# Splitting W_o's quadrant sums and W_A's pieces once, early, and keeping the halves in DRAM

## The chip, the cores and the metric

The kernel runs on one core of a Trainium2 chip. The metric is the device time of one execution in microseconds (us). Of the kernel before there are three runs: 1529.68, 1530.45 (the median) and 1532.38 us. Beside the times there is one profiled execution, whose trace gives every instruction of every engine and every DMA.

The engines are named as in the profile: PE is the tensor engine (PEld its weight loads), DVE the vector engine, ACT the scalar engine, POOL the GpSimd engine, and SP the sync engine, whose work here is to issue DMAs. Each engine runs its instructions in the order of its own queue.

## The reference

One layer of a streaming encoder on 2048 prompt tokens and 32 sample tokens, width 1024, all in float32:

```python
h = rmsnorm(x, ln_g)
(q, k, v, gate_a, b_gate, c_gate, u_in, gate_c, merge_a, merge_c) = split(h @ w_in)
attn = chunked sliding-window attention(q, k, v) with sinks      # 8 q heads, 2 kv heads
y_a = (attn * silu(gate_a)) @ w_attn_out                         # W_A, 512 -> 1024
y_c = (b_gate * conv3(c_gate * u_in) * silu(gate_c)) @ w_conv_out  # W_B
r = x + (sigmoid(merge_a) * y_a + sigmoid(merge_c) * y_c) @ w_o    # W_o, 1024 x 1024
out = r + sigmoid(r @ w_ple_gate) * (p @ w_ple_proj)               # W_pg, W_pp
```

The caches of k and v and the last rows of the convolution's input are outputs too.

## The kernel before, in words

**Halves.** Every matmul is made of three: an operand is split into a high half (a cast by ACT to the matmul's own float32 form) and a low half (source minus high half, by DVE), and high x high, high x low and low x high are added up in one bank. `split` (L228) does this for a tile. A weight piece is a tile of 128 x 512 (256 KB in float32); its two halves lie together in a tile `w` of 512 KB, of which there are five (`WB`).

**Seven products.** The large matrix products are computed in Strassen's way with seven products of quadrants instead of eight, numbered 1 to 7. Products 1, 2 and 4 use a weight quadrant as it is; 7, 5, 6 and 3 use sums of quadrants, named `sc`, `a21`, `a11` and `a12` in the code, and kept at places 0 to 3 (`WS`, L338).

**First phase (some 0 to 850 us of the trace).** The combined projection `h @ W_in`, by 21 groups `g` of output columns: of the first token half (steps `(0, g, product)`), then of the second. In steps whose key stands in `sums_at` (L1201), `quad_sums(x, n)` (L368) is called for the second phase: it loads the four quadrants of columns `n` of W_o (`x = UO`, 50) or W_pg (`x = UPG`, 58), makes the four sums by four adds on DVE and stores them to DRAM (`quad_sum`, `qs` in the profile) by four DMAs on POOL. Its five tiles come from the pool of temporaries `tp`. This phase is written in program order, but its start and the second phase are issued in an order that the kernel's own planner finds when the program is built: it keeps clocks for the engines (`now`, `busy`), costs per instruction (L104, L120) and counts of free tiles (`live`, `limit`), and issues a step when it fits. Between these, the framework's scheduler orders the first phase's instructions by when their tiles come free.

**Second phase.** `plan` (L307 to L318) lists its units: `yB` (W_B), `pp` (W_pp), `yA` (W_A, by token blocks 0 to 3 and column pieces), and `B` units, the seven products of W_o and W_pg for the first token half (named `b050_...` and `b058_...`: half, matrix, columns, product) and for the second (`b150_...`, `b158_...`). Attention (L1343) runs beside them, tile by tile, started at fixed amounts of PE work; its transposes and products stand between the units' matmuls on PE. Rows of activations are split into `xb` pairs (L1645). Outputs are evicted into tiles `c` (`big_done`, L1698) and combined on DVE, then brought together with x or r by an accumulating DMA on POOL and stored by SP.

**Weights of the second phase.** `worder` (L325) lists every weight piece in the order of use. `next_loads` (L1924) runs whenever the planner's clock moves: it lets SP load raw pieces, up to 11 ahead of the one in use (`LOOK`), into one of eight tiles `wr` (tag `wf`): from `in_wu` where a piece is a quadrant, from `quad_sum` where it is a sum (L1954). When one has landed, a `w` tile is free and ACT is not busy, `split_w` (L1910) splits it. W_A's pieces are used once per token block, so each is loaded and split four times; each sum of W_o twice.

## Time and profile before

| | |
|---|---|
| Median of three runs | 1530.45 us |
| Profiled execution, its own time | 1533.35 us |
| Span from first to last instruction | 1531.6 us |
| Mean granted PE clock | 0.991 |
| PE, DVE, ACT, POOL busy | 98%, 80%, 53%, 24% |
| DMA moved | 346.89 MB, mean 226 GB/s |

A busy share is the time in which at least one instruction of the engine was in flight. Matmuls overlap each other, so a duration in a PE row is longer than the distance between two of them; the distance is read from counts (so many matmuls in so many us). In rows of waits stand the engine, tile and line that waited, what it waited for, the sum, the number of waits and the longest. In rows of stretches each engine's busy time is followed by its number of instructions; then come the granted clock, the mean busy share of the 16 DMA engines and the rate. [...]

### The profile page before, as it was taken

The numbers are of one execution on the slowest core, as the hardware profiler recorded it, in microseconds if no ns is written. First come the engines' busy times: TensorE is split into PE (matmuls) and PEld (weight loads), VectorE is DVE, ScalarE is ACT, GpSimd is POOL, SyncE is SP. The second block draws the span as 40 slices with busy tenths as digits, with TensorE's granted clock in tenths as the row PEclk, the third lists the DMA queues.
The fourth block names the chain that finished last, engine by engine and source line by source line (L and its number), as shares of the span: only waits on it lengthen the run. The fifth ranks groups of instructions, "written<-read, shape, count | busy, mean of one in ns | idle before, by whom it ended". The sixth has DMA issues, their size and how long they took to land.

```text
span 1531.6 us, 27944 instructions
## 1 busy us (share of the span) xinstructions
PE 1500.7 (98%) x9553; PEld 1355.8 (89%) x9553; DVE 1227.2 (80%) x2330; ACT 818.2 (53%) x1933; POOL 370.5 (24%) x534
## 2 busy tenths in 40 slices
...
GB/s 340 151 276 342 313 295 216 282 344 266 241 279 257 315 149 195 112 132 119 175 192 187 265 234 205 210 186 231 239 127 184 187 128 300 312 240 145 254 143 288
DMA packets 199231, 346.89 MB, mean 226 GB/s; under 512 B 23728, under 2 KB 57072, under 8 KB 199088
## 3 DMA queue, kind: packets, MB, share of 16 engines
...
HBM read 227.66 MB, written 117.46 MB: 225 GB/s over the span
## 4 chain that ended last, share of the span: by engine, by line
PE 38%; DVE 7%; ACT 3%; DMA 2%; issue 2%; SPq 0%; ACTq 0%; DVEq 0%
PE b L158 17%; PE yB L158 5%; PE yA L158 5%; PE O L158 2%; PE S L158 2%; DVE c L158 1%; PE la L749 1%; PE pp L158 1%; PE a L611 1%; PE a L613 1%; PE a L616 1%; PE PT L158 1%; DVE w L158 1%; DVE xb_l L158 1%; DVE tk L158 1%
## 5 line engine op out<-in xcount | busy, mean ns | idle before, releaser
L158 PE MATMUL b<-xb_h,w 128*128 128x264 f32 (+1 forms) x1344 | 315.3, 326 | 7.2 <-DVE c L158 4.5
L158 PEld LDWEIGHTS b<-xb_h,w 128*128 128x128 f32 x1344 | 225.1, 190 | 27.6 <-DVE c L158 4.2
L613 PE MATMUL a<-x_l,w 128*128 128x264 f32 (+1 forms) x744 | 228.1, 320 | 0.0
L611 PE MATMUL a<-x_h,w 128*128 128x264 f32 (+1 forms) x744 | 227.1, 319 | 0.0
L158 PE MATMUL b<-xb_l,w 128*128 128x264 f32 (+1 forms) x672 | 218.4, 325 | 0.8 <-DVE xb_l L158 0.8
L616 PE MATMUL a<-x_h,w 128*128 128x264 f32 (+1 forms) x744 | 201.6, 320 | 0.0
L229 ACT CAST w<-wr 128x512 fp32r<-128x512 f32 (+1 forms) x180 | 110.2, 619 | 105.7 <-PE c L616 35.4
L230 DVE TENSOR_TENSOR w<-wr,w 128x512 fp32r<-128x512 f32 (+1 forms) x180 | 136.1, 767 | 33.9 <-ACT w L229 32.7
L158 ACT CAST w<-wr 128x512 fp32r<-128x512 f32 x168 | 103.5, 623 | 105.7 <-PE b L158 53.0
L611 PEld LDWEIGHTS a<-x_h,w 128*128 128x128 f32 x744 | 139.9, 188 | 10.5
L613 PEld LDWEIGHTS a<-x_l,w 128*128 128x128 f32 x744 | 139.7, 188 | 10.7
L158 PEld LDWEIGHTS b<-xb_l,w 128*128 128x128 f32 x672 | 127.8, 190 | 10.8 <-DVE xb_l L158 1.6
L616 PEld LDWEIGHTS a<-x_h,w 128*128 128x128 f32 x744 | 125.0, 188 | 10.7
L158 DVE TENSOR_TENSOR w<-wr,w 128x512 fp32r<-128x512 f32 x168 | 117.8, 706 | 14.1 <-ACT w L158 13.4
L749 PE MATMUL la<-x_h,w 128*128 128x264 f32 x516 | 112.2, 285 | 1.9 <-ACT w L229 1.2
L613 PE MATMUL c<-x_l,w 128*128 128x512 f32 (+1 forms) x336 | 110.7, 339 | 0.0
L611 PE MATMUL c<-x_h,w 128*128 128x512 f32 (+1 forms) x336 | 110.6, 340 | 0.0
L229 ACT CAST w<-a 128x512 fp32r<-128x512 f32 x82 | 49.7, 620 | 98.1 <-DVE a L360 31.5
L616 PE MATMUL c<-x_h,w 128*128 128x512 f32 (+1 forms) x336 | 100.4, 340 | 0.0
L810 DVE SCALAR_TENSOR_TENSOR u<-u,c 128x264 f32<-128x264 f32 (+1 forms) x125 | 59.4, 506 | 44.5 <-ACT u L805 30.0
L158 PE MATMUL yB<-ycs_h,w 128*128 128x264 f32 (+1 forms) x384 | 91.0, 326 | 0.0
L805 ACT COPY u<-a 128x264 f32<-128x264 f32 (+1 forms) x114 | 47.4, 437 | 80.7 <-PE a L616 80.7
...
## 6 DMA issues: line engine op xcount, KB each, us to landing
wr<-in_wu SPq DMA_DIRECT2D x177, 256.0 KB, 4.1
a<-in_wu SPq DMA_DIRECT2D x116, 256.0 KB, 5.3
wr<-ws SPq DMA_DIRECT2D x74, 256.0 KB, 3.5
wr<-qs SPq DMA_DIRECT2D x64, 256.0 KB, 3.9
ws<-a POOLq DMA_DIRECT2D x63, 256.0 KB, 4.0
qs<-a POOLq DMA_DIRECT2D x24, 256.0 KB, 5.8
...
```

The lines of the kernel that those rows point to most:

```text
L158: return f(**kw)
L229: nc.scalar.copy(out=hi, in_=src)
L230: nc.vector.tensor_tensor(out=lo, in0=src, in1=hi.bitcast(F32), op=sub)
L611: nc.tensor.matmul(out=ps[:, :cn], lhsT=w[:, 0, k], rhs=x[0][:, c0:c0 + cn], start=first and k == 0, stop=False, skip_group_check=True)
L613: nc.tensor.matmul(out=ps[:, :cn], lhsT=w[:, 0, k], rhs=x[1][:, c0:c0 + cn], start=False, stop=False, skip_group_check=True)
L616: nc.tensor.matmul(out=ps[:, :cn], lhsT=w[:, 1, k], rhs=x[0][:, c0:c0 + cn], start=False, stop=k == 3, skip_group_check=True)
L749: nc.tensor.matmul(out=ps[:, :m], lhsT=w[:, a, k], rhs=r[:, cols], start=q in "ABG" and j == 0 and e == 0, stop=j == 1 and e == 2, skip_gr ...
L805: nc.scalar.copy(out=t[:, c0:c0 + cn], in_=ps[:, :cn])
L810: nc.vector.scalar_tensor_tensor(out=t[:, c0:c0 + cn], in0=t[:, c0:c0 + cn], scalar=-1.0, in1=ps[:, :cn], op0=mul, op1=sub)
```

## The change

`quad_sum` of W_o now keeps two halves per sum, 128 x 2 x 512, and a new array `wa_split` keeps the eight W_A pieces in the same way (`wa` in the profile). `quad_sums` takes its tiles from a new pool of five tiles (`zp`) that lives during the first phase, and is done in two parts: the loads at step `(0, g, 6)`, the adds, splits and stores at `(0, g, 7)`. For W_o each sum is split at once (`store_split`: an ACT cast into a temporary, a DVE subtraction in place) and stored by two DMAs of 256 KB; W_pg's sums are stored unsplit. `piece_split` loads, splits and stores a W_A piece. W_o's sums are called for at g = 1, 3, 5, 7, W_pg's now at 9, 11, 13, 15, W_A's pieces at 2, 4, ... 16; before, the eight sums stood at g = 1 to 8.

In the second phase, `stored` says of a piece whether its halves lie in DRAM: the 32 uses of W_A's pieces and the 32 uses of W_o's sums. For these `next_loads` skips the raw load, and when a `w` tile is free SP loads both halves into it by one DMA of 512 KB; `split_w` is not called.

The order of the instructions moves in three places that matter. The first is the start-up, on SP and on DVE. `wr` are raw weight pieces, `a0` the quadrants of the first group's sums, `b1` and `sq1` rows of x and their squares, `a11_50_0` and the like the quadrants of W_o's first columns. SP before:

```order
L158 DMA wr7_405<-in_wu 128x512
L158 DMA wr8_426<-in_wu 128x512
L158 DMA a0_0_488<-in_wu 128x512
L158 DMA a0_1_489<-in_wu 128x512
L158 DMA a0_2_490<-in_wu 128x512
L158 DMA a0_3_491<-in_wu 128x512
L158 DMA wr9_644<-in_wu 128x512
L158 DMA wr10_652<-in_wu 128x512
```

and with the change:

```order
L158 DMA wr7_413<-in_wu 128x512
L158 DMA wr8_434<-in_wu 128x512
L372 DMA a11_50_0_1125<-in_wu 128x512
L372 DMA a21_50_0_1127<-in_wu 128x512
L158 DMA a0_0_496<-in_wu 128x512
L372 DMA a22_50_0_1129<-in_wu 128x512
L372 DMA a12_50_0_1131<-in_wu 128x512
L158 DMA a0_1_497<-in_wu 128x512
L158 DMA a0_2_498<-in_wu 128x512
L158 DMA a0_3_499<-in_wu 128x512
L372 DMA wa_0_1299<-in_wu 128x512
L158 DMA wr9_652<-in_wu 128x512
```

W_o's four quadrants and the first W_A piece now stand among the start-up's loads; before, the quadrants' loads came fifteen loads behind `wr9`, and no W_A piece was loaded in this phase. DVE before, at the same place:

```order
L158 TENSOR_TENSOR sq1_0_466<-sq1_0_466,sq1_4_560 128x512
L158 TENSOR_TENSOR w5_606<-wr5_309,w5_606 128x512
L158 TENSOR_TENSOR w6_610<-wr6_376,w6_610 128x512
L158 TENSOR_TENSOR w7_615<-wr7_405,w7_615 128x512
L158 TENSOR_TENSOR sc0_636<-a0_0_488,a0_1_489 128x512
L158 TENSOR_TENSOR sq1_0_466<-sq1_0_466,sq1_5_570 128x512
L158 TENSOR_TENSOR a0_1_489<-a0_1_489,a0_2_490 128x512
L158 TENSOR_TENSOR sq1_0_466<-sq1_0_466,sq1_6_582 128x512
L158 TENSOR_TENSOR a0_0_488<-a0_0_488,a0_1_489 128x512
L158 TENSOR_TENSOR sq1_0_466<-sq1_0_466,sq1_7_594 128x512
```

and with the change:

```order
L158 TENSOR_TENSOR sq1_0_474<-sq1_0_474,sq1_3_555 128x512
L387 TENSOR_TENSOR a21_50_0_1127<-a21_50_0_1127,a22_50_0_1129 128x512
L158 TENSOR_TENSOR sq1_0_474<-sq1_0_474,sq1_4_568 128x512
L158 TENSOR_TENSOR w5_614<-wr5_317,w5_614 128x512
L158 TENSOR_TENSOR w6_618<-wr6_384,w6_618 128x512
L158 TENSOR_TENSOR w7_623<-wr7_413,w7_623 128x512
L387 TENSOR_TENSOR a11_50_0_1125<-a11_50_0_1125,a21_50_0_1127 128x512
L158 TENSOR_TENSOR sc0_644<-a0_0_496,a0_1_497 128x512
L158 TENSOR_TENSOR sq1_0_474<-sq1_0_474,sq1_5_578 128x512
L387 TENSOR_TENSOR a12_50_0_1131<-a12_50_0_1131,a11_50_0_1125 128x512
L158 TENSOR_TENSOR a0_1_497<-a0_1_497,a0_2_498 128x512
L158 TENSOR_TENSOR sq1_0_474<-sq1_0_474,sq1_6_590 128x512
```

One add (`sc_50_0`) stands one row ahead of these; `sq1_7` follows two rows behind. The four adds of W_o's first sums have come in ahead of it.

The second place is W_o of the first token half. `nm` and `tt` are steps of attention, `w396` a weight's low half, `xb050_6_3_l` the low half of an activation row. DVE before:

```order
L158 SCALAR_TENSOR_TENSOR tk0_3_12693<-tk0_3_12693,tk1_3_13382 128x512
L158 TENSOR_REDUCE nm_20_13665<-S_20_0_13629 128x2
L158 TENSOR_REDUCE nm_20_13665<-S_20_1_13634 128x2
L158 TENSOR_TENSOR w396_13654<-wr396_13343,w396_13654 128x512
L158 TENSOR_TENSOR tt2_3_13658<-pq2_3_13639,ab2_3_13647 128x1024
L158 TENSOR_TENSOR tt2_3_13658<-pkv2_3_13644,ab2_3_13647 128x256
L158 TENSOR_REDUCE ss2_3_13678<-sq_10098 128x10
L158 TENSOR_TENSOR c11_050_3_2_12927<-c11_050_3_2_12927,b050_3_1_0_13618 128x512
L158 SCALAR_TENSOR_TENSOR xb050_6_3_l_13692<-tk0_3_12693,xb050_6_3_h_13691 128x512
```

and with the change:

```order
L158 TENSOR_REDUCE nm_20_13691<-S_20_1_13678 128x2
L158 TENSOR_TENSOR tk1_3_13452<-tk1_7_13531,tk1_3_13452 128x512
L158 SCALAR_TENSOR_TENSOR tk0_3_12781<-tk0_3_12781,tk1_3_13452 128x512
L158 TENSOR_TENSOR c11_050_2_2_12988<-c11_050_2_2_12988,b050_2_1_0_13653 128x512
L158 TENSOR_TENSOR tt2_3_13725<-pq2_3_13707,ab2_3_13715 128x1024
L158 TENSOR_TENSOR tt2_3_13725<-pkv2_3_13712,ab2_3_13715 128x256
L158 TENSOR_REDUCE ss2_3_13747<-sq_10230 128x10
L158 TENSOR_TENSOR c11_050_3_2_13020<-c11_050_3_2_13020,b050_3_1_0_13701 128x512
L158 RECIPROCAL se_20_13717<-se_20_13717 128x4
L158 SCALAR_TENSOR_TENSOR xb050_6_3_l_13736<-tk0_3_12781,xb050_6_3_h_13735 128x512
```

The weight's split ahead of `tt2_3` is gone. The planner, whose engines have less to do, also puts attention elsewhere. PE before, where the sample tile's probabilities are transposed (`PT_s`):

```order
L158 MATMUL b058_0_1_0_14530<-xb058_6_2_l_14612,w415_14470 128x512
L158 MATMUL b058_0_1_0_14530<-xb058_6_2_h_14611,w415_14470 128x512
L158 MATMUL PT_s_0_14685<-cst_69,Ps_14521 128x128 x2
L158 MATMUL PT_s_0_14685<-cst_69,Ps_14521 64x128
L158 MATMUL b058_0_1_0_14530<-xb058_6_3_h_14645,w415_14470 128x512
```

and with the change:

```order
L158 MATMUL b050_3_5_0_14372<-xb050_5_2_h_13969,w406_14181 128x512
L158 MATMUL PT_s_0_14412<-cst_69,Ps_14283 128x128 x2
L158 MATMUL PT_s_0_14412<-cst_69,Ps_14283 64x128
L158 MATMUL b050_3_5_0_14372<-xb050_5_2_l_13970,w406_14181 128x512
L158 MATMUL b050_3_5_0_14372<-xb050_5_2_h_13969,w406_14181 128x512
```

`PT_s` stood among W_pg's units (`b058`) and stands now among W_o's (`b050`).

The third place is SP where the second token half begins; `w441` to `w444` are the W_A pieces of units `yA2`, `tk2` their rows, `out_yT` stores of results. Before:

```order
L158 DMA wr447_15755<-in_wu 128x512
L158 DMA wr448_15765<-in_wu 128x512
L158 DMA out_yT<-c11_058_0_1_14559 128x512
L158 DMA wr449_15786<-in_wu 128x512
L158 DMA tk2_4_15791<-z_t0_4_104 128x528
L158 DMA wr450_15795<-in_wu 128x512
L158 DMA out_yT<-c11_058_1_1_14609 128x512
L158 DMA out_yT<-c11_058_2_1_14802 128x512
L158 DMA tk2_5_15847<-z_t0_5_105 128x528
L158 DMA wr451_15849<-in_wu 128x512
```

and with the change:

```order
L158 DMA w441_15826<-wa4_149 128x1024
L158 DMA pp0_3_15845<-z_pp7_91 128x512
L158 DMA wr449_15847<-in_wu 128x512
L158 DMA out_yT<-c11_058_0_1_14679 128x512
L158 DMA w442_15856<-wa5_150 128x1024
L158 DMA tk2_4_15879<-z_t0_4_104 128x528
L158 DMA wr450_15881<-in_wu 128x512
L158 DMA w443_15886<-wa6_151 128x1024
L158 DMA out_yT<-c11_058_1_1_14725 128x512
L158 DMA tk2_5_15922<-z_t0_5_105 128x528
L158 DMA wr451_15924<-in_wu 128x512
L158 DMA w444_15930<-wa7_152 128x1024
```

Loads of 128 x 1024 into `w` tiles now stand between the rows and the stores; the raw pieces of `yA2` that were loaded ahead of this place are gone.

The diff:

```diff
--- before.py
+++ after.py
@@ -363,18 +363,45 @@
         for p, i in WS.items():
             nc.gpsimd.dma_start(out=wsum[g][:, i], in_=sums[g][p])
 
-    quad_sum = {(x, n): dram.tile([P, 4, 4, P], F32, tag=f"qs{x}_{n}", name=f"qs{x}_{n}") for x in (UO, UPG) for n in range(4)}
+    quad_sum = {(x, n): dram.tile([P, 4, 1 + (x == UO), 4 * P], F32, tag=f"qs{x}_{n}", name=f"qs{x}_{n}")
+                for x in (UO, UPG) for n in range(4)}
+    wa_split = [dram.tile([P, 2, 4 * P], F32, tag=f"wa{n}", name=f"wa{n}") for n in range(8)]
+
+    def quad_load(name, u, e):
+        t = zp.tile([P, 4 * P], F32, tag="z", name=name)
+        nc.sync.dma_start(out=t.rearrange("p (a b) -> p a b", a=4), in_=wu[u, :, 4 * e:4 * e + 4, :])
+        return t
+
+    def store_split(dst, t, name):
+        h = tmp(f"h{name}", F32R)[:, :512]
+        split(h, t.bitcast(F32R), t)
+        nc.gpsimd.dma_start(out=dst[:, 0], in_=h.bitcast(F32))
+        nc.gpsimd.dma_start(out=dst[:, 1], in_=t)
 
     def quad_sums(x, n):
-        t = {}
-        for name, u, e in (("a11", n, 0), ("a21", n + 4, 0), ("a22", n + 4, 1), ("a12", n, 1)):
-            t[name] = tmp(f"{name}_{x}_{n}")[:, :512].rearrange("p (a b) -> p a b", a=4)
-            nc.sync.dma_start(out=t[name], in_=wu[x + u, :, 4 * e:4 * e + 4, :])
-        t["sc"] = tmp(f"sc_{x}_{n}")[:, :512].rearrange("p (a b) -> p a b", a=4)
+        t = {name: quad_load(f"{name}_{x}_{n}", x + u, e)
+             for name, u, e in (("a11", n, 0), ("a21", n + 4, 0), ("a22", n + 4, 1), ("a12", n, 1))}
+        yield
+        t["sc"] = zp.tile([P, 4 * P], F32, tag="z", name=f"sc_{x}_{n}")
         for o, v, w in (("sc", "a11", "a21"), ("a21", "a21", "a22"), ("a11", "a11", "a21"), ("a12", "a12", "a11")):
             nc.vector.tensor_tensor(out=t[o], in0=t[v], in1=t[w], op=add)
         for p, o in ((7, "sc"), (5, "a21"), (6, "a11"), (3, "a12")):
-            nc.gpsimd.dma_start(out=quad_sum[x, n][:, WS[p]], in_=t[o])
+            if x == UO:
+                store_split(quad_sum[x, n][:, WS[p]], t[o], f"{p}_{x}_{n}")
+            else:
+                nc.gpsimd.dma_start(out=quad_sum[x, n][:, WS[p], 0], in_=t[o])
+
+    def piece_split(n):
+        t = quad_load(f"wa_{n}", UY + n, 0)
+        yield
+        store_split(wa_split[n], t, f"wa_{n}")
+
+    def stored(key):
+        if key[0] == "q" and key[3] == 0:
+            return wa_split[key[2] - UY]
+        if key[0] == "B" and key[2] == UO and key[4] in WS:
+            return quad_sum[key[2:4]][:, WS[key[4]]]
+        return None
 
     def raw_key(key):
         if key[0] == "q":
@@ -1198,7 +1225,12 @@
         refills[at_step[at_]] = p
     after = {at_step[1, pairs_[9], 2, "C"]: sets[0]}
     after.update({at_step[1, sets[i - 1][-1], 5]: sets[i] for i in range(1, len(sets))})
-    sums_at = {(0, 1 + 2 * n + e, 6): (x, n) for n in range(4) for e, x in enumerate((UO, UPG))}
+    zpool = tc.tile_pool(name="zpool", bufs=5)
+    zp = zpool.__enter__()
+    sums_at = {(0, 1 + 2 * n, 6): quad_sums(UO, n) for n in range(4)}
+    sums_at.update({(0, 9 + 2 * n, 6): quad_sums(UPG, n) for n in range(4)})
+    sums_at.update({(0, 2 + 2 * n, 6): piece_split(n) for n in range(8)})
+    sums_at.update({(0, g, 7): v for (_, g, _), v in sums_at.items()})
     prep = [at_step[0, g, 7] for g in range(7, G)]
     for i, todo in enumerate(steps):
         if i < NS:
@@ -1214,7 +1246,7 @@
         if i in prep:
             next(X1, None)
         if todo[0] in sums_at:
-            quad_sums(*sums_at[todo[0]])
+            next(sums_at[todo[0]], None)
         if i in after:
             load_second_products(after[i])
         if i in refills:
@@ -1224,6 +1256,7 @@
             refill(refills[i])
     nc.gpsimd.dma_start(out=cpo, in_=halo)
     nc.gpsimd.dma_start(out=cso, in_=halo_out)
+    zpool.__exit__(None, None, None)
     xpool.__exit__(None, None, None)
 
 
@@ -1941,6 +1974,9 @@
 
         while n_load[0] < min(len(worder), used[0] + LOOK) and busy["Y"] < now[0] + 0.5:
             i = n_load[0]
+            if stored(worder[i]) is not None:
+                n_load[0] += 1
+                continue
             fin[0] = 0.0
             if room["wf"] < 1:
                 break
@@ -1951,16 +1987,27 @@
                 uu, e = raw_key(key)
                 eY.dma_start(out=t, in_=wu[uu, :, 4 * e:4 * e + 4, :])
             else:
-                eY.dma_start(out=t, in_=quad_sum[key[2:4]][:, WS[key[4]]])
+                eY.dma_start(out=t, in_=quad_sum[key[2:4]][:, WS[key[4]], 0].rearrange("p (a b) -> p a b", a=4))
             raw_of[i] = t
             landed[i] = fin[0] + 0.5
             n_load[0] += 1
         while n_split[0] < len(worder) and room["w"] > 0:
             i = n_split[0]
-            if landed.get(i, 1e9) > now[0] or busy["S"] >= now[0] + (0.3 if i > used[0] + 2 else 1.5):
-                break
-            room["w"] -= 1
-            go(split_w(i))
+            src = stored(worder[i])
+            if src is not None:
+                if busy["Y"] >= now[0] + 0.5:
+                    break
+                room["w"] -= 1
+                w = wp.tile([P, 2, 4, P], F32R, tag="w", name=f"w{i}")
+                W2[i] = w[:, 0], w[:, 1]
+                fin[0] = 0.0
+                eY.dma_start(out=w.bitcast(F32).rearrange("p a b c -> p a (b c)"), in_=src)
+                w_ready[i] = fin[0] + 0.5
+            else:
+                if landed.get(i, 1e9) > now[0] or busy["S"] >= now[0] + (0.3 if i > used[0] + 2 else 1.5):
+                    break
+                room["w"] -= 1
+                go(split_w(i))
             n_split[0] += 1
 
     work = [0.0]
```

## The prediction

> **What bounds the kernel now.** I read the page's head first, then busy time by stretches, then the waits of the tensor engine (PE) in the stretches where it is not full, then the place of one wait.
>
> ```profile
> span 1531.6 us, 27944 instructions
> ...
> PE 1500.7 (98%) x9553; PEld 1355.8 (89%) x9553; DVE 1227.2 (80%) x2330; ACT 818.2 (53%) x1933; POOL 370.5 (24%) x534
> ```
>
> PE is busy for 1500.7 of 1531.6 us. The change removes no matmul, so it can only win from some 31 us of idle PE and from time at half clock. The next rows (us, busy time by engine, clock, DMA share, GB/s) tell where these lie.
>
> ```profile
> core 0: us, PE busy (x) PEld busy (x) DVE busy (x) ACT busy (x) POOL busy (x), PEclk, DMA share, GB/s
> 50.00:450.00 400.00, 399.91 (x1736) 322.65 (x1735) 308.23 (x508) 174.78 (x328) 109.76 (x203) 1.00 0.79 276
> 1021.00:1195.00 174.00, 168.13 (x900) 141.44 (x899) 155.29 (x301) 115.52 (x331) 46.38 (x50) 0.99 0.75 199
> 1195.00:1311.00 116.00, 108.69 (x552) 90.34 (x551) 106.22 (x206) 83.37 (x231) 24.70 (x25) 0.94 0.75 213
> 1311.00:1385.00 74.00, 74.00 (x608) 73.91 (x607) 53.83 (x101) 34.23 (x74) 13.84 (x17) 1.00 0.93 259
> 1385.00:1432.00 47.00, 47.00 (x389) 47.00 (x388) 38.92 (x76) 20.33 (x36) 6.91 (x8) 1.00 0.70 173
> 1432.00:1525.00 93.00, 93.00 (x765) 93.00 (x765) 73.46 (x135) 44.12 (x83) 13.81 (x16) 1.00 0.82 232
> ```
>
> 1021 to 1195 holds W_A and W_o of the first token half (yA0, yA1, b50), 1195 to 1311 its W_pg (b58), 1311 to 1432 W_A and W_o of the second half. The first phase's first half (50 to 450) and the second half of the tokens lose nothing. The loss is 5.87 us in 1021 to 1195 and 7.31 in 1195 to 1311, beside half clock: 0.01 x 174 and 0.06 x 116 of clock, about 2 and 7 us at full-rate equivalent, partly inside the same gaps. Exactly there VectorE (DVE) is 89% and 92% busy, against 77 to 83% where PE is full. What ended PE's gaps, in the first of these stretches and in the second:
>
> ```profile
> PE b L158 <- ACT xb_h L158: 2.8, 1, 2.8
> PE pq L158 <- ACT E L158: 1.4, 1, 1.4
> PE b L158 <- DVE c L158: 0.9, 1, 0.9
> PE PT L158 <- ACT P L158: 0.5, 1, 0.5
> PE b L158 <- DVE xb_l L158: 0.3, 1, 0.3
> ```
>
> ```profile
> PE b L158 <- DVE c L158: 3.6, 2, 3.3
> PE PT_s L158 <- ACT Ps L158: 3.2, 1, 3.2
> PE b L158 <- DVE xb_l L158: 0.5, 1, 0.5
> ```
>
> Half of them name ScalarE (ACT), but the timeline around the 2.8 us shows that ACT itself was held up. Rows are start, duration, instruction, idle time before it and its cause.
>
> ```profile
> 1120.13 0.68 DVE L158 TENSOR_TENSOR w<-wr,w 128x512 fp32r<-128x512 f32 x1
> 1120.73 1.22 DVE L158 TENSOR_TENSOR tt<-pq,ab 128x1024 f32<-128x1024 f32 x1
> ...
> 1122.31 0.86 ACT L158 CAST VH<-pkv 64x64 fp32r<-64x64 f32 x4 [4.36 <-DVE tt L158]
> ...
> 1123.68 1.15 ACT L158 ACTIVATE xb_h<-tk 128x512 fp32r<-128x512 f32 x2
> ...
> 1124.37 0.50 PE L158 MATMUL b<-xb_h,w 128*128 128x512 f32 x1 [2.75 <-ACT xb_h L158]
> ```
>
> DVE runs without a gap and is late with tt, an attention step; ACT stands 4.36 us in front of VH; the cast of xb_h behind it is late; PE waits 2.75 us. Just ahead of tt DVE made a weight's low half (w, 0.68), of the kind the change removes. So the bound of this stretch is DVE's in-order queue, not PE, ACT or DMA.
>
> **The change part by part.**
>
> *Splits taken out of the second phase.* 64 of its weight splits go (32 W_A pieces, 32 W_o sums): one ACT cast and one DVE subtraction each. Their price, in 1021 to 1195:
>
> ```profile
> L158 DVE TENSOR_TENSOR w<-wr,w 128x512 fp32r<-128x512 f32 x44 | 32.3, 737 | 0.9 <-ACT w L158 0.5
> ```
>
> Issued back to back, such rows start 0.60 us apart (1120.13 and 1120.73 above); 32.3/44 gives 0.73. Of the 44, 16 belong to raw W_o, W_pg or other pieces that stay, by the program's order 28 go (4 of yA0, whose other splits lie earlier, 8 of yA1, 16 of W_o): 28 x 0.73 = 20.4 us of DVE's 155.3, which leaves 78% of 174 us. The 1195 to 1311 stretch loses only 4 splits (the first of yA2), 2.9 us. But the planner fills what becomes free: the sample tile's attention with its PT_s, which stood in W_pg and made the 3.2 us wait, is now issued inside W_o. So part of the 20 us comes to the second stretch's help. Splits of the second token half (another 28) are worth nothing, since PE is full there.
>
> What is this worth? Bounds: nothing, if new places fall late in the same way; and all of 13.2 us of waits plus the half clock at most. Stretches with DVE at 77 to 83% have no waits at all, which speaks for much of it. In 1021 to 1195 I take 4 of 5.9 us; in 1195 to 1311 4.5 of 7.3 (the PT_s wait whole, the other 3.3 us in part), since there DVE stays above 85%. Of the half clock I take 2.5 us. **Gain 11 us**, bounds 0 and 18.
>
> The Trainium skill, page TensorE: Matmul & The Clock Gate, section HAM oscillation, says that an idle stretch of about one 3.4 us window puts PE at half rate, at a penalty of half the throttled time. The trace agrees: 0.06 x 116 is 7 us of missing clock beside two gaps of 3.2 and 3.3 us. By that rule my clock term could be 3.5 + 1 us instead of 2.5, and the sum 2 us better.
>
> *The first phase gets 24 splits, 8 loads and 32 more stores.* The rows of the same work there, then two stretches of DMA:
>
> ```profile
> L230 DVE TENSOR_TENSOR w<-a,w 128x512 fp32r<-128x512 f32 x82 | 55.3, 687 | 16.0 <-ACT w L229 15.7
> ...
> L229 ACT CAST w<-a 128x512 fp32r<-128x512 f32 x82 | 49.7, 620 | 98.1 <-DVE a L360 31.5 <-PE c L616 22.6 <-PE a L616 22.3
> ```
>
> ```profile
> 320.00:340.00 20.00, 20.00 (x87) 16.15 (x87) 15.07 (x24) 8.82 (x16) 7.17 (x14) 1.00 1.00 352
> ...
> 20.00:25.00 5.00, 5.00 (x25) 3.99 (x24) 3.46 (x6) 4.83 (x10) 1.08 (x2) 1.00 1.04 410
> ```
>
> 24 x 0.69 = 16.6 us of DVE and 24 x 0.62 = 14.9 of ACT go into 400 us, of which DVE has 92 and ACT 225 idle. 40 x 256 KB is 10.5 MB, 26 us at 410 GB/s; the DMA engines have 0.21 x 400 = 84 us. The UPG sums move later, so the added bytes fall mostly on 240 to 400 us; at 320 to 340 PE was full with the DMA share at 1.00. I take 0; bounds 0 and 5 us (one 20 us stretch at 1.00 with a quarter more bytes). Cover: the raw weights that are loaded a group ahead.
>
> *Start-up.* With a pool of their own the first quadrant sums no longer wait for a temporary. Their four loads and the first piece now go out on SP among the start-up's, ahead of the later a0 pieces and wr9, and their four adds on DVE ahead of the last sq add. That add releases PE's pr:
>
> ```profile
> 37.30 1.89 DVE L158 TENSOR_TENSOR w<-wr,w 128x512 fp32r<-128x512 f32 x3
> ...
> 42.11 0.68 DVE L158 TENSOR_TENSOR sq<-sq,sq 128x512 f32<-128x512 f32 x1
> ```
>
> ```profile
> 44.46 0.95 PE L158 MATMUL pr<-ones,sq 128*128 128x1 f32 x8
> ```
>
> The sq add ends at 42.79, 1.67 us before PE comes to pr. Four adds x 0.60 = 2.4 us come ahead of it, and some tenths for the landing of a22: PE stands about **1 us**. Bounds 0 and 3 (five loads of 0.26 MB at 410 GB/s are 3.2 us for whatever is loaded behind them).
>
> *Loads of 512 KB into the matmuls' own tiles.* Each stored pair is read on SP into one of five w tiles, when its last user has ended. Before, raw pieces came into eight other tiles and were split later. The lookahead falls from 13 pieces to 5. A piece lasts PE 12 x 20/87 = 2.76 us (512 columns) or 24 x 47/389 = 2.90 (2 x 264), so a load goes out about four pieces, 11 to 11.6 us, ahead of its use. How long do loads take, in 1311 to 1385 and (last row) in 1021 to 1195?
>
> ```profile
> q1 hardware_dynamic: 8621, 14.47, 56.9%
> q0 software_dynamic: 2468, 4.59, 35.2%
> ...
> wr<-in_wu SPq DMA_DIRECT2D x13, 256.0 KB, 6.9
> ...
> wr<-qs SPq DMA_DIRECT2D x12, 256.0 KB, 5.0
> ```
>
> ```profile
> wr<-qs SPq DMA_DIRECT2D x23, 256.0 KB, 3.9
> ```
>
> q1 moves 14.47 MB in 0.569 x 74 = 42.1 us, 344 GB/s, so 256 KB more are 0.76 us: 4.7 and 7.7 us against 11, and nothing is late by latency alone. By volume 1311 to 1385 is the tight place: now 25 weight loads (6.6 MB); after, by the program's order, 16 pairs and 8 raw pieces (10.5 MB). 3.9 MB are 11.4 us, and the engines have 0.07 x 74 = 5.2 us left: short by 6 us. The lead holds 11.6 - 7.7 = 3.9 of these, and from 1385 the share is 0.70. I take **2 us** of stalls, bounds 0 and 10 (the shortage whole, with some half clock).
>
> The Trainium skill, page DMA: Bandwidth & Descriptors, section Anatomy of one DMA, gives some 2.0 us plus bytes over 436 GB/s for one transfer, an estimate of 3.2 us for 512 KB. By that this term is nothing and the sum 2 us better; the 6.9 us row for half the bytes shows a queue that the rule leaves out, so I hold to the row.
>
> *SP's queue.* These loads wait on SP for a tile, and stores and attention's loads stand behind them. SP waits today as well:
>
> ```profile
> SPq L158 <- DVE w L158: 105.5, 39, 13.0
> ...
> SPq L158 <- DMA c<-in_xT: 12.7, 8, 4.9
> ```
>
> 105.5 us in 1021 to 1311 for raw tiles that DVE has to free; now for w tiles that PE frees, which comes earlier. Behind a z_r store that waits 4.9 us for its accumulation a w load would still have 11 - 4.7 - 4.9 = 1.4 us. I take 0, in the bounds of the term before.
>
> **Sum.** The profiled execution took 1533.35 us (span 1531.6). -11 + 0 + 1 + 2 = -8 gives 1525.3 for it; it lay 2.9 above the median 1530.45, so the forecast is **1522.5 us**.
>
> **Rivals.**
>
> *The waits only move.* The planner packs attention into the freed time until DVE is again late elsewhere. For it: that is how PT_s moved; W_pg keeps its splits. Against: DVE's total falls. A gain of 3 us, less the 3 of start-up and loads: 1530.5.
>
> *The w loads come late.* Where yA2 and yA3 run, each unit reads 512 KB of weight beside its rows; once a load lands later than 11.6 us after its tile is free, PE waits for each one. It decides if the 6.9 us row grows by more than 4.7 us. If 16 units wait 1 us each, with three half-clock windows of 3.4 us (5 us lost), that is 21 us against 11: 1530.5 - 11 + 1 + 21 = 1541; with half the units waiting, 1531. For it: the DMA share of 0.93 and the 6 us shortage. Against: PE did not lose 0.1 us there so far.
>
> *The start-up or the first phase slips.* A load behind the five new ones, or a weight at 300 to 360 us, comes 3 to 5 us late and half of the gain in W_pg fails: 1530.5 - 6 + 8 = 1532.5. Against: PE's 399.91 of 400 us.
>
> *Everything falls into place.* All waits and the half clock go, loads are in time: 1530.5 - 18 + 1 = 1513.5.
>
> **How the numbers follow.** Forecast 0.48, everything falls into place 0.10, waits move 0.20, late w loads 0.15, start-up or first phase 0.07. The forecast's own range is 1517 to 1528. The whole range takes in the good case and the milder part of the late loads: 1513 to 1535, with about one in ten left out on either side. About 0.2% (3 us) can be told from no change. Faster: the good case, most of the forecast and a little of the moved waits, 0.58. Same: the rest of these, 0.22. Slower: late loads, part of the slip, 0.20.
>
> **What would show it.** Right: PE's waits in W_o of the first half fall to about 2 us and DVE's share there to about 80%; no PT_s wait in W_pg; PE full from 1311 on, pr about 1 us late. Wrong: PE rows that wait for DMA w<-wa or w<-qs; a landing of over 11 us for them; waits on c or xb_h as long as before in W_pg; gaps between 50 and 450 us.

## The result, and the profile after

Four runs of the changed kernel took 1543.32 to 1548.48 us, median 1544.3; four of the kernel before, on the same chip, had a median of 1530.6. The ratio is 1.0093, with a 95% interval of 1.0072 to 1.0114. The forecast was 1522.5, its range 1513 to 1535. The profiled execution took 1544.87 us (span 1543.1, 11.5 more than before). The medians are 13.7 us apart, the profiled executions 11.5, since that of the kernel before lay 2.9 above its median; the account below is of the 11.5.

The head of the page after:

```profile
span 1543.1 us, 27852 instructions
...
PE 1503.1 (97%) x9553; PEld 1355.9 (88%) x9553; DVE 1197.3 (78%) x2290; ACT 794.1 (51%) x1893; POOL 388.2 (25%) x566
```

DVE works 30 us less, PE as much as before in a longer span. Busy time by stretches, with the columns of the prediction; the stretches are shifted to the same work (W_A and W_o of the first token half, its W_pg, then yA2 onwards), and the first phase is cut at 240 and 360 us. A DMA share can exceed 1 because it adds up the times of the packets, and these overlap: in both traces up to 24 packets are in flight at once on the 16 engines.

```profile
core 0: us, PE busy (x) PEld busy (x) DVE busy (x) ACT busy (x) POOL busy (x), PEclk, DMA share, GB/s
50.00:240.00 190.00, 189.91 (x815) 152.34 (x815) 156.12 (x256) 90.98 (x174) 59.95 (x114) 1.00 0.76 270
240.00:360.00 120.00, 110.86 (x457) 88.19 (x456) 92.39 (x148) 44.30 (x89) 38.94 (x73) 0.96 0.88 305
360.00:450.00 90.00, 90.00 (x389) 72.76 (x388) 58.81 (x104) 39.98 (x70) 26.94 (x51) 1.00 0.88 305
1034.00:1208.00 174.00, 171.22 (x933) 144.78 (x932) 145.02 (x291) 106.29 (x320) 49.25 (x52) 0.99 0.90 250
1208.00:1314.00 106.00, 103.41 (x542) 85.76 (x541) 97.40 (x190) 80.72 (x227) 23.26 (x23) 1.00 0.75 204
1314.00:1388.00 74.00, 66.00 (x519) 64.80 (x519) 35.27 (x69) 17.39 (x34) 12.09 (x14) 0.98 1.03 311
```

W_pg's stretch is 106 us long instead of 116 and runs at full clock. Two stretches that had been full now have holes: 240 to 360 lacks 9.1 us of PE, 1314 to 1388 lacks 8.0. The waits of PE follow: in the start-up (from 5 us on; the kernel before has one such wait there, of 1.3 us), from 240 to 360, from 1314 to 1388, in W_A and W_o (1034 to 1208), and in W_pg (1208 to 1314):

```profile
PE pr L158 <- DVE sq L158: 2.7, 2, 1.4
```

```profile
PE a L638 <- ACT u L832: 5.9, 2, 3.5
PE b L638 <- ACT w L229: 3.2, 1, 3.2
```

```profile
PE yA L158 <- DMA w<-wa: 6.5, 3, 4.8
PE b L158 <- DVE xb_l L158: 1.3, 1, 1.3
```

```profile
PE pq L158 <- DMA zq<-z_q: 2.1, 1, 2.1
PE b L158 <- DVE xb_l L158: 0.7, 1, 0.7
```

```profile
PE S L158 <- ACT w L158: 1.2, 1, 1.2
PE b L158 <- DVE xb_l L158: 0.9, 2, 0.6
PE pqt L158 <- DVE se L158: 0.3, 1, 0.3
PE pk L158 <- DVE kr L158: 0.2, 1, 0.2
```

To compare many kernels, one measure serves below: **PE's loss**, the distance between the starts of consecutive matmuls less the distance at full rate for their width, as the traces show it (0.231 us for 512 columns, 0.121 for 264, 0.109 for up to 128), summed over a stage. It holds waits and half clock alike, and each figure comes from one profiled execution. The stages are set by the first matmul of each kind, so they move with the work.

| Stage | before | after | difference |
|---|---|---|---|
| Start-up, 0 to 60 us | 7.9 | 11.0 | +3.1 |
| First phase, first token half (60 to 441, after to 459) | 3.75 | 18.5 | **+14.7** |
| First phase, second token half (to 858 / 874) | 9.2 | 8.0 | -1.2 |
| yB and pp (to 1022 / 1034) | 10.1 | 6.75 | -3.3 |
| W_A, W_o, W_pg of the first half (to 1311 / 1314) | 25.1 | 12.5 | **-12.6** |
| 90 us from the first yA2 unit on | 0.8 | 11.4 | **+10.6** |
| The rest | 0.8 | 0.9 | +0.1 |

The differences add up to 11.4 of the 11.5 us. The gain is there, about as large as forecast; it is paid back on both sides of it. (W_A to W_pg became only 9.6 us shorter, 280.2 instead of 289.8, since 2.9 us more of attention's matmuls now stand in it.)

### The profile page after: what moved, and what is told of

It reads as the page before. It is cut to its first block, busy times and chain, and to the rows that moved or that the text cites. A ratio compares the mean times of both kernels' runs of the same rounds, so it can differ in the third digit from the quotient of the medians.

```text
span 1543.1 us, 27852 instructions
## 1 busy us (share of the span) xinstructions
PE 1503.1 (97%) x9553; PEld 1355.9 (88%) x9553; DVE 1197.3 (78%) x2290; ACT 794.1 (51%) x1893; POOL 388.2 (25%) x566
## 4 chain that ended last, share of the span: by engine, by line
PE 77%; DMA 8%; DVE 7%; issue 4%; ACT 3%; POOL 1%; SPq 0%; DVEq 0%; POOLq 0%; ACTq 0%
PE b L158 16%; PE a L643 6%; PE a L638 6%; PE a L640 6%; PE la L776 5%; PE yB L158 4%; PE yA L158 4%; PE c L638 3%; PE c L643 3%; PE c L640 3%; PE lc L776 3%; PE O L158 2%; DMA w<-wa 2%; DVE c L158 1%; PE S L158 1%
## 5 line engine op out<-in xcount | busy, mean ns | idle before, releaser
L158 PE MATMUL b<-xb_h,w 128*128 128x264 f32 (+1 forms) x1344 | 311.0, 323 | 0.0
L640 PEld LDWEIGHTS a<-x_l,w 128*128 128x128 f32 x744 | 140.4, 189 | 10.7
L643 PEld LDWEIGHTS a<-x_h,w 128*128 128x128 f32 x744 | 125.8, 189 | 11.2 <-DVE w L230 0.4
L158 ACT CAST w<-wr 128x512 fp32r<-128x512 f32 x104 | 63.8, 620 | 92.5 <-PE b L158 52.9
L158 PE MATMUL yA<-ac_h,w 128*128 128x264 f32 (+1 forms) x384 | 93.2, 328 | 6.7 <-DMA w<-wa 6.5
L776 PEld LDWEIGHTS la<-x_h,w 128*128 128x128 f32 x516 | 86.9, 188 | 1.9 <-ACT w L229 1.4
```

The lines of the kernel that those rows point to most:

```text
L158: return f(**kw)
L640: nc.tensor.matmul(out=ps[:, :cn], lhsT=w[:, 0, k], rhs=x[1][:, c0:c0 + cn], start=False, stop=False, skip_group_check=True)
L643: nc.tensor.matmul(out=ps[:, :cn], lhsT=w[:, 1, k], rhs=x[0][:, c0:c0 + cn], start=False, stop=k == 3, skip_group_check=True)
L776: nc.tensor.matmul(out=ps[:, :m], lhsT=w[:, a, k], rhs=r[:, cols], start=q in "ABG" and j == 0 and e == 0, stop=j == 1 and e == 2, skip_gr ...
```

## The experiments

Fifteen kernels ran. The table has each one's median, its ratio to the runs of the kernel before on its own chip (their medians lay between 1526.8 and 1530.6), and PE's loss, in its profiled execution, in four stages: start-up, first phase (first token half), W_A to W_pg, and 90 us from yA2.

| Run | us | ratio (95%) | start-up | first phase | W_A..W_pg | yA2 |
|---|---|---|---|---|---|---|
| before | 1530.6 | | 7.9 | 3.75 | 25.1 | 0.8 |
| changed | 1544.3 | 1.0093 (1.0072-1.0114) | 11.0 | 18.5 | 12.5 | 11.4 |
| e1 | 1545.4 | 1.0113 (1.0097-1.0129) | 10.6 | 18.1 | 13.1 | 11.4 |
| e2 | 1549.0 | 1.0134 (1.0116-1.0152) | 11.7 | 19.8 | 12.9 | 10.9 |
| e3 | 1543.4 | 1.0093 (1.007-1.0116) | 9.4 | 19.3 | 14.4 | 7.6 |
| e4 | 1544.7 | 1.0106 (1.0091-1.0121) | 10.7 | 12.35 | 14.5 | 6.9 |
| e5 | 1539.4 | 1.0054 (1.0032-1.0076) | 6.7 | 15.7 | 13.6 | 10.8 |
| e6 | 1535.3 | 1.0043 (1.003-1.0057) | 6.75 | 16.5 | 13.5 | 6.8 |
| e7 | 1539.8 | one run | 11.2 | 18.5 | 12.9 | 5.6 |
| e8 | 1541.3 | one run | 11.85 | 12.2 | 13.3 | 11.0 |
| e9 | 1537.9 | one run | 7.8 | 12.65 | 13.1 | 11.8 |
| e10 | 1530.1 | 1.0003 (0.9993-1.0014) | 6.55 | 3.8 | 12.8 | 10.7 |
| **e11** | **1525.8** | **0.9978 (0.9966-0.9991)** | 6.7 | 3.8 | 13.2 | 6.8 |
| e12 | 1530.9 | 1.0018 (1.0006-1.0031) | 6.1 | 4.0 | 24.9 | 0.8 |
| e13 | 1541.25 | 1.0086 (1.0057-1.0115) | 6.2 | 14.85 | 22.3 | 0.7 |
| e14 | 1534.2 | 1.0042 (1.0022-1.0061) | 6.8 | 7.95 | 22.6 | 0.8 |
| e15 | 1549.5 | 1.0138 (1.0056-1.0221) | 6.7 | 16.4 | 22.7 | 0.6 |

**First theory: a queue.** The first gap of the first phase looks like one. SP, ACT and PE of the changed kernel, each from its timeline (start, duration, instruction, idle time and its cause):

```profile
266.18 4.83 SPq L372 DMA_DIRECT2D a<-in_wu  x2
...
274.22 0.36 SPq L348 DMA_DIRECT2D wr<-in_wu  x1
```

```profile
282.80 0.62 ACT L229 CAST w<-wr 128x512 fp32r<-128x512 f32 x1 [10.19 <-DMA wr<-in_wu]
```

```profile
283.47 0.79 PE L638 MATMUL b<-x_h,w 128*128 128x512 f32 x1 [3.21 <-ACT w L229]
```

Between two loads of a W_pg sum (L372) SP stood still for a z tile, which had to wait for its store to land; the raw weight behind them went out at 274.22, ACT waited 10.19 us for it, and PE 3.21 us for ACT. e1 takes these loads out of that place, e2 out of SP's queue.

**e1: the two tables swapped.**

```diff
-    sums_at.update({(0, 9 + 2 * n, 6): quad_sums(UPG, n) for n in range(4)})
-    sums_at.update({(0, 2 + 2 * n, 6): piece_split(n) for n in range(8)})
+    sums_at.update({(0, 2 + 2 * n, 6): quad_sums(UPG, n) for n in range(4)})
+    sums_at.update({(0, 9 + n, 6): piece_split(n) for n in range(8)})
```

> The changed kernel with two tables swapped: the W_pg sums are made at the even groups 2 to 8, where they stood before the change, and the eight W_A pieces one per group from 9 to 16. Same loads, same stores, same splits. The changed kernel is 11.5 us of span longer than the one before: PE is 3.0 us late by the third matmul bank of the start-up, 16.5 late at 754 us, 14.0 late at the first yB unit, 3.0 late at the first yA2 unit and 11.5 at the end. Theory Q (queue): the 13 us of the first phase come from SP's in-order queue, where loads of the W_pg sums wait for one of five z tiles and hold the raw weights of the next groups behind them, in the stretch where SP also loads the xT rows; one piece per group needs one tile and seldom waits, so the loss falls to 0 to 3 us, total about 1531 to 1534. Theory B (bytes): the added reads and stores are too much wherever they lie; the even groups 2 to 8 then carry both sums and lose there what the later groups gain, total 1540 to 1545. Theory D (VectorE and ScalarE): the 24 splits are too much; no change of the sum of the loss, 1544.

**e2: the new loads on POOL's queue.**

```diff
     def quad_load(name, u, e):
-        nc.sync.dma_start(out=t.rearrange(...), in_=wu[u, :, 4 * e:4 * e + 4, :])
+        nc.gpsimd.dma_start(out=t.rearrange(...), in_=wu[u, :, 4 * e:4 * e + 4, :])
```

> The changed kernel with the 40 new loads (32 quadrants of the sums, 8 pieces) issued on POOL's queue instead of SP's, at the same steps. Bytes, splits and z tiles are the same. Theory Q: raw weights no longer stand behind these loads on SP, the gaps of PE at 280, 310 and 334 us go, the first phase loses 0 to 4 instead of 13 us, total 1532 to 1536, if POOL's own stores do not get late. Theory B: the same transfers share the same 16 DMA engines, the gaps stay, 1542 to 1546.

Theory Q missed in both. In e1 the gaps moved with the sums, to 138 to 215 us and one at 336; in e2 they came at 217 to 320 us, and the loss is as large. The gap at 280 us is a queue's, but taking the queue away brings other gaps: theory Q falls as the cause of the whole. The changed kernel's other two long gaps, at 310 and 334 us, read differently. There ACT waits for a sum of the first phase's own quadrants on DVE:

```profile
310.54 1.14 ACT L229 CAST w<-a 128x512 fp32r<-128x512 f32 x2 [5.17 <-DVE a L360]
```

```profile
336.44 0.62 ACT L229 CAST w<-a 128x512 fp32r<-128x512 f32 x1 [7.26 <-DVE a L360]
```

Ahead of the first of these DVE is busy for 17.00 of the 17 us from 296 to 313, and the cast of a W_A piece (0.61 us at 311.59) then stands on ACT ahead of the copy `u` for which PE waits.

**e3: the second token half reads W_A raw.**

```diff
     def stored(key):
-        if key[0] == "q" and key[3] == 0:
+        if key[0] == "q" and key[3] == 0 and key[1] < 2:
```

> The changed kernel with the W_A pieces read as halves only for the first token half; for the second token half (yA2, yA3) they are raw loads of 256 KB that are split, as before the change. The first phase is untouched. Theory L (the 512 KB loads come late there): the waits of yA2 for DMA w<-wa go, the stretch from the first yA2 unit to the end is again about 220 us instead of 228.7, total about 1536. Rival M (moved wait): the 16 splits that return, four of them in W_pg of the first half, where VectorE is the bound, take back 3 to 6 us, or PE waits in yA2 for VectorE's w instead: total 1540 to 1544.

Half right: the waits for `w<-wa` are gone and yA2 loses 3.8 us less, but 7.6 us stay, with a new name. PE's wait from 1300 to 1360 us, and a row of DVE there:

```profile
PE b L158 <- DVE xb_l L158: 4.4, 2, 2.6
```

```profile
1332.25 0.77 DVE L158 SCALAR_TENSOR_TENSOR tk<-tk,yA 128x264 f32<-128x264 f32 x2 [4.10 <-DMA tk<-z_t]
```

Now it is the rows of z_t that land late. The DMA engines were full (share 1.07 from 1320 to 1350, 314 GB/s).

**e4: no W_A pieces.**

```diff
-    sums_at.update({(0, 2 + 2 * n, 6): piece_split(n) for n in range(8)})
 ...
     def stored(key):
-        if key[0] == "q" and key[3] == 0:
+        if False:
```

> The changed kernel without the W_A pieces: they are neither split and stored in the first phase nor read as halves in the second; the W_o sums are. Theory Q: the W_pg sums still stand at groups 9 to 15 with four loads for five z tiles, so most of the first phase's loss stays (8 to 13 of 13 us); yA2 loses nothing (-8.6); the second phase's first half gets 12 splits back in yA0 and yA1 and four in W_pg, 12 us of VectorE, and loses some 4 to 6 of its gain of 10.9: total 1536 to 1542. Theory B: without 2 MB of reads and 4 MB of stores in groups 2 to 16 the first phase loses at most half, total 1530 to 1535.

The first phase still loses 8.6 us more than before the change, so the pieces with their 16 stores account for some 6 of 14.7; neither theory's total (1536 to 1542, 1530 to 1535) holds. yA2 was to lose nothing without the 512 KB loads of W_A, and loses 6.9 us, much as in e3. In the second phase the 16 splits put back into the first token half cost 2 us in W_A to W_pg. (Its loss in yB and pp is 5.4 us larger, but that stage differs by as much between runs with the same second phase: 6.75 in the changed kernel, 11.2 in e10.)

**e5, e6: the sums in temporaries, as before the change.** In `quad_sums` the five tiles come from `tmp`, loads and adds stand in one step, and the tables are those of e1; the high halves take z tiles. e6 has e3's line too.

> The changed kernel with the sums made as before the change: in the shared temporaries, loads and adds in one step, W_o's at groups 1, 3, 5, 7 and W_pg's at 2, 4, 6, 8. The splits of W_o's sums, their stores, the eight W_A pieces (groups 9 to 16) and the second phase's reading stay; only the high halves and the pieces use the five z tiles. So what is undone is the z tiles under the sums, the loads that run ahead on SP and the late place of the W_pg sums. By time that PE loses against full rate, the kernel before lost 7.9 us in the first 60 us and 3.75 in the rest of the first phase, the changed one 11.0 and 18.5, and with the loads of the sums on POOL's queue 11.7 and 19.8, with the W_pg sums early 10.6 and 18.1, without the pieces 10.7 and 12.4. Theory Z (the z tiles and the early loads, through whichever in-order queue they stand in): the start-up loses 8 and the first phase 4 to 7 us, total 1528 to 1532 against 1527 to 1530 of the kernel before. Theory D (the 24 added splits and the 40 added stores themselves): the first phase still loses 13 to 18 us, total 1540 to 1544.

> As the run with the sums in temporaries, and the W_A pieces of the second token half read raw (256 KB) and split, as before the change. If theory Z holds and the loss of yA2 is the 4 us smaller that the run with raw pieces showed (7.6 against 11.4 us), this is 3 to 4 us below the former: 1524 to 1528, a little faster than the kernel before. If the first phase loses its 13 us whatever holds the sums, 1536 to 1540.

This undoes the start-up's 3 us whole: with the loads no longer running ahead, it loses 6.7. The first phase keeps 12 of its 14.7 us, with its gaps at other places (176 to 261 us). So the loads that run ahead into the z tiles are the cause of the one; a loss like the other comes without them too. e6 adds to this what e3 showed: yA2 loses 6.8 instead of 10.8 us.

**e7: 4.2 MB less around yA2.**

```diff
-        eY.dma_start(out=yT[k * P:(k + 1) * P, cols], in_=t)
+        if u["s"]:
+            eY.dma_start(out=yT[k * P:(k + 1) * P, cols], in_=t)
```

> The changed kernel leaves out the 16 stores of yT for the first token half (256 KB each, 4.2 MB; these outputs are not written), which stand on SP's queue between 1240 and 1340 us. Nothing else is changed. With raw pieces PE still lost 7.6 us from the first yA2 unit on, waiting for rows that come late (tk from z_t), at a DMA share of 1.07 from 1290 to 1350. Theory T (the transfers of W_pg's end and of yA2 together are more than the DMA engines move by the time PE is there, so a faster W_pg is paid back): without these 4.2 MB of some 20 the loss from yA2 on (11.4 us) falls to 0 to 4 us. Rival L (five w tiles are too short a lead for 512 KB, whatever the load): the waits for w<-wa stay at 5 us or more, and the loss at 7 to 11 us.

Between the two: yA2's loss falls from 11.4 to 5.6 us, and 3.0 us of waits for `w<-wa` stay. Together with e3 this speaks for about 4 us from the 512 KB loads and a larger part from the transfers that W_pg leaves in the queue when PE gets to yA2 sooner. Whether these stores cost by their bytes or by their places on SP (last section), e7 does not separate.

**e8, e9: no splitting.** In `store_split` both stores take the sum itself, in the changed kernel (e8) and in e5 (e9):

```diff
-        h = tmp(f"h{name}", F32R)[:, :512]
-        split(h, t.bitcast(F32R), t)
-        nc.gpsimd.dma_start(out=dst[:, 0], in_=h.bitcast(F32))
+        nc.gpsimd.dma_start(out=dst[:, 0], in_=t)
```

> The changed kernel leaves out the 24 casts and 24 subtractions that make the stored halves: both stores take the sum or the piece itself, so what W_A and W_o multiply in the second phase is not the weights. Loads, z tiles, places and bytes of all stores are the same. Theory D1 (the added work on ScalarE and VectorE makes the first phase late): its loss from 60 us to the end of the first half, 18.5 us, falls to 4 to 8 us. Theory D2 (loads, tiles and bytes make it late): it stays at 13 to 19 us, with the gaps at 280, 310 and 334 us.

> The kernel with the sums in temporaries at the old steps, again without the 24 casts and 24 subtractions (both stores take the sum or the piece; what is multiplied later is not the weights). With the splits this first phase lost 15.7 us, 12 more than before the change, in gaps at 176, 247 and 261 us that name ScalarE's cast of a weight. D1: without them 4 to 7 us. D2 (the 32 added stores, the eight piece loads and their tiles): 12 to 16 us.

Without any added cast or subtraction the first phase still loses 12.2 and 12.65 us, 8.5 and 8.9 more than before the change, so most of the loss comes without the added splits. But e8 fits neither of its theories: the gaps at 280, 310 and 334 us are gone, and the loss lies earlier. e8 from 60 to 360 us:

```profile
60.00:240.00 180.00, 175.01 (x738) 138.01 (x737) 144.79 (x237) 76.31 (x148) 64.08 (x120) 0.99 0.86 304
240.00:360.00 120.00, 120.00 (x519) 96.83 (x518) 93.13 (x147) 48.37 (x94) 34.24 (x64) 1.00 0.80 275
```

From 240 to 360 us, where the changed kernel loses most, PE is full in e8. So the changed kernel's own three gaps need the splits, or the order of work that comes with them.

**e10, e11: the same work elsewhere.** With e5's temporaries for all, W_pg's sums stay at groups 2 to 8; the others go where the DMA engines have room. e11 has e3's line too.

```diff
+    late = [steps[i][0] for i in range(len(steps)) if steps[i][0][0] == 1]
+    sums_at.update({late[82 + 9 * n]: piece_split(n) for n in range(8)})
+    sums_at.update({late[232 + 15 * n]: quad_sums(UO, n) for n in range(4)})
```

> All of the change's work stays, at other places: the W_pg sums in temporaries at groups 2 to 8 as before the change; the eight W_A pieces and W_o's four sums in temporaries between about 550 and 650 us and 760 and 830 us, where VectorE is 75% and 65% busy and the DMA engines 46% and 64%, instead of 50 to 360 us. The second phase reads as in the changed kernel. If what the first phase loses comes from added work beside its first half's loads (rows of x, xT, raw weights), whichever engine: the first phase loses 4 to 6 us, the start-up 7, the second phase's first half keeps its gain of 12 to 16, yA2 keeps its loss of 11: total 1522 to 1528 against 1527 to 1530 of the kernel before. If the losses only move with the work: 1535 or more.

> As the former, and the second token half reads its W_A pieces raw (256 KB) and splits them. yA2's loss 6.8 to 7.6 instead of 11 us, so 3 to 5 us below the former: 1518 to 1524. If the losses only move with the work: 1531 or more.

The first phase's loss is gone (3.8), the second token half of the first phase loses no more than before (7.9 and 7.0 against 9.2), and the gain stays. e10 is a tie with the kernel before, since yA2 still costs 10.7 us; e11 is **faster than both kernels**, by 0.2% than the one before (0.9978, 0.9966 to 0.9991). Both medians lie some 2 us above the ranges that were expected. e11's profile lost 48.3 us in all, against 57.6. The medians are 3.6 us apart, fewer than the two profiled executions (1524.1 and 1533.35 us), of which that of the kernel before lay 2.9 above its median and that of e11 1.7 below its own.

**e12, e13, e14: one part alone, in the kernel before.** e12 gets the 24 splits and 8 piece loads without a store; e13 stores each of its 32 sums twice; e14 does so with an eighth of the bytes.

```diff
 # e13
             nc.gpsimd.dma_start(out=quad_sum[x, n][:, WS[p]], in_=t[o])
+            nc.gpsimd.dma_start(out=spare[x, n][:, WS[p]], in_=t[o])
 # e14
+            nc.gpsimd.dma_start(out=spare[x, n][:16, WS[p]], in_=t[o][:16])
```

> The kernel before the change, to which only the added split work is given: the 16 sums of W_o and the eight W_A pieces (loaded one per group from 9 to 16) are split by a cast and a subtraction into five z tiles, and the halves are dropped; no store is added, the second phase is that of the kernel before. The first phase after 60 us lost 3.75 us before the change, 15.7 with everything in it (sums in temporaries), 12.65 without the splits. If splits and piece loads cost by themselves: 7 us or more. If the stores are what costs: 4 to 5 us.

> The kernel before the change, whose 32 sums of W_o and W_pg are each stored a second time, right behind the first store and on the same queue (POOL's), to a spare place in DRAM: 32 more stores of 256 KB, as many as the change adds, at groups 1 to 8; no split, no piece load. If the added stores make the first phase late (POOL's queue, or bytes beside the loads): loss from 60 us to its end 10 us or more instead of 3.75. If not: 4 to 6 us, and the cost of the first phase is only in the sum of loads, splits and stores.

> As the run in which the kernel before the change stores its 32 sums a second time, but the second stores carry 16 of the 128 rows (32 KB instead of 256 KB): as many instructions on POOL's queue at the same places, an eighth of the bytes. The full second stores took the loss of the first phase after 60 us from 3.75 to 14.85 us. If the bytes are what makes raw weights and rows land late: 4 to 7 us. If POOL's queue (0.54 us for each store it issues, and what waits behind them) is: 11 to 15 us.

The stretch from 50 to 240 us of e12 and of e13:

```profile
50.00:240.00 190.00, 189.81 (x817) 152.07 (x817) 165.91 (x273) 99.95 (x197) 55.93 (x102) 1.00 0.82 287
```

```profile
50.00:240.00 190.00, 182.09 (x771) 143.99 (x770) 148.78 (x244) 78.25 (x151) 71.18 (x131) 0.99 0.83 303
```

e12 has DVE busy for 166 of 190 us, and PE is full. e13 has less DVE work (149 us) and more transfers (303 GB/s), and PE lacks 7.9 us. So the 24 splits and the 8 loads cost this stage nothing by themselves (+0.3 us; e12 as a whole is 0.2% slower, and loses 1.7 us more in the second token half of the first phase), and the 32 stores, with the order of work that they bring, cost 11.1. With an eighth of the bytes 4.2 of the 11.1 remain, all from 210 to 240 us, where e13 loses as much; the gap at 159 is gone. This speaks for the bytes in most of it. It does not prove it, because the program also orders SP's loads differently: in e13 the loads of W_o's third sums stand between the four quadrants of a first-phase group, in e14 ahead of the last of them, in the kernel before behind all four.

**e15: four more tiles for the raw weights,** under e13's stores.

```diff
-        sc = quad(f"sc{g}")
+        sc = scp[0].tile([P, 4, P], F32, tag="sc", name=f"sc{g}") if scp else quad(f"sc{g}")
```

> The kernel before the change with its 32 sums stored twice, as in the run that lost 14.85 us in the first phase after 60 us; now the tile sc, one of the five that the sums of a first-phase group take from the eight raw tiles, comes from four tiles of its own. In the former run the four raw quadrants of group 6 no longer stood together on SP: the loads of W_o's third sums had come between the first two and the last two (order of the program), the last was issued at 150.8 us instead of 144 to 146, and DVE's third sum ended at 162.5 instead of 152.7, 3.9 us after PE wanted it. Theory R (raw tiles: a raw quadrant's tile is free only when its sum's store has landed, the added stores delay these on POOL, and the raw loads of the next groups go out late, behind others): with four tiles more the raw loads stand ahead again and the loss falls to 4 to 7 us with all 32 stores in place. Theory B (bytes as such): it stays at 11 to 15 us.

The gap at 159 us went, and others came, the longest at 215 us behind rows of x. PE's and ACT's waits there:

```profile
PE rps L499 <- DVE dg L497: 4.3, 1, 4.3
```

```profile
ACT xt L515 <- DMA xt<-in_x: 8.0, 5, 4.7
```

The loss is 16.4 us, so these four tiles do not buy it back; the order of the loads changed here too. Whichever transfer is late, a raw weight or a row, the 32 full stores beside it are what e13 and e15 have in common.

## Why the prediction was wrong

**The splits taken out of the second phase (-11): right.** PE's loss falls by 12.6 us from W_A to W_pg, within the bounds 0 to 18; the 3.3 us in yB and pp are not counted on, since e1 and e10, with the same second phase, do not show them. It came as argued: no wait for `c` or `PT_s` is left, W_A and W_o wait 2.8 us (forecast about 2), DVE is busy there for 145.02 of 174 us, 83% (forecast about 80). The waits fell by 7.8 us (5.9 to 2.8 in W_A and W_o, 7.3 to 2.6 in W_pg), where 8.5 were taken. The half clock was under-priced: W_pg's clock went from 0.94 to 1.00, and the waits leave 4.8 of the 12.6 us for it, where 2.5 were taken. By the rule of the Trainium skill (page TensorE: Matmul & The Clock Gate, section HAM oscillation) that term was 4.5, nearer to the measurement. (The prediction gives DVE's share where PE is full as 77 to 83%; its row for 1311 to 1385 shows 73%, which changes nothing in the sum.)

**The first phase (0, bounds 0 to 5): wrong, and the step that decided.** It measured +14.7 us, or +13.5 with the 1.2 regained later. The step that failed is "40 x 256 KB is 10.5 MB, 26 us at 410 GB/s; the DMA engines have 0.21 x 400 = 84 us". The rate is not what failed. The idle 21% is a mean over 400 us, and the stores were counted as bytes that nobody waits for. The rival "the start-up or the first phase slips", with a chance of 0.07, came with twice its 8 us: 16.6 with the start-up. From 100 to 160 us, first before the change, then in e12, in e13 and in e10:

```profile
100.00:160.00 60.00, 60.00 (x260) 48.48 (x259) 45.20 (x73) 22.99 (x41) 22.69 (x42) 1.00 0.94 345
```

```profile
100.00:160.00 60.00, 60.00 (x261) 48.54 (x260) 50.59 (x82) 27.43 (x49) 23.23 (x43) 1.00 0.98 348
```

```profile
100.00:160.00 60.00, 59.34 (x256) 47.56 (x254) 40.03 (x65) 19.10 (x34) 28.90 (x54) 1.00 1.03 388
```

```profile
100.00:160.00 60.00, 60.00 (x259) 48.49 (x259) 39.98 (x63) 21.34 (x39) 18.91 (x35) 1.00 0.83 287
```

The DMA engines had 6% left there, not 21%. With the stores they are full for 60 us on end, and e13's first long gap (4.0 us, at 159) follows; at 0.98 PE is still full. e13 shows that added stores alone cost 11.1 us there, e10 that the change's work costs nothing in stretches where the kernel before left the engines this much room (e10 itself runs there at 0.60 and 0.93, with PE full):

```profile
550.00:650.00 100.00, 100.00 (x824) 100.00 (x823) 75.19 (x147) 43.84 (x97) 29.00 (x45) 1.00 0.46 145
750.00:850.00 100.00, 99.36 (x816) 99.15 (x815) 65.20 (x134) 55.06 (x116) 21.41 (x24) 1.00 0.64 211
```

In the changed kernel the added transfers stand elsewhere in part, and its gaps come at 280 to 340 us. Before the change and after it:

```profile
240.00:290.00 50.00, 50.00 (x218) 40.30 (x217) 41.57 (x67) 16.63 (x30) 13.49 (x26) 1.00 0.66 227
290.00:360.00 70.00, 70.00 (x302) 56.53 (x302) 55.48 (x88) 28.92 (x50) 23.17 (x43) 1.00 0.93 321
```

```profile
240.00:290.00 50.00, 46.79 (x197) 37.28 (x196) 39.15 (x63) 21.82 (x50) 15.93 (x30) 0.97 0.87 301
290.00:360.00 70.00, 64.08 (x262) 50.90 (x261) 53.24 (x85) 22.48 (x40) 23.01 (x44) 0.95 0.88 307
```

Up to 290 us, with the first gap, the share rose from 0.66 to 0.87; behind it, with the other two, it fell from 0.93 to 0.88. So the share, as a mean over such a stretch, does not explain those two. That the place of the work is the cause is shown by e10: elsewhere the same work is free. Which part of it makes which gap (transfers, DVE's queue, or the order of work) stays open; e4 and e8 each take the loss down, by some 6 us, without the pieces and without the splits.

The step beside it held in the kernel before: "24 x 0.69 = 16.6 us of DVE and 24 x 0.62 = 14.9 of ACT" go in free (e12: +0.3). In the changed kernel they count (e8: 6.2 us less without them). The cover that was named, raw weights loaded a group ahead, did not hold: in the first gap shown above the weight was cast at 282.80, right at its landing.

**Start-up (+1, bounds 0 to 3): right in place, too small.** PE waited 1.34 us at `pr` behind `sq`, as worked out. Some 3 us at half clock followed, a loss of about 1.5 that was not priced, and the sum is +3.1. It comes from the loads that run ahead: the runs that have them lose 9.4 to 11.9 us in the start-up, the others 6.1 to 7.9.

**Loads of 512 KB (+2, bounds 0 to 10): the rival "the w loads come late" came instead.** It measured +10.6, the size of that rival with half the units waiting (half of 21 us). The arithmetic "short by 6 us" was sound; the step that failed is "the lead holds 11.6 - 7.7 = 3.9 of these". The landing grew to 10 or 11 us, not 7.7. Transfers issued from 1273 to 1343 us, and those of before from 1270 to 1340:

```profile
w<-wa SPq DMA_DIRECT2D x8, 512.0 KB, 10.1
...
tk<-z_t SPq DMA_DIRECT2D x8, 264.0 KB, 11.1
```

```profile
tk<-z_t SPq DMA_DIRECT2D x8, 264.0 KB, 7.9
```

The cause that the rival named holds only in part: e3 gives the 512 KB some 4 us. The rest was in no term. The engines were full there before the change too:

```profile
1280.00:1311.00 31.00, 31.00 (x178) 26.79 (x178) 27.18 (x52) 24.82 (x72) 9.42 (x11) 1.00 1.05 299
1311.00:1341.00 30.00, 30.00 (x248) 29.91 (x247) 21.18 (x42) 14.16 (x33) 6.05 (x8) 1.00 1.07 307
```

A W_pg that ends about 10 us sooner, counted from the first W_A unit, reaches yA2 with its own stores still in the queue: without 4.2 MB of them yA2 loses 5.8 us less (e7), and with raw pieces, as before the change, it still loses 7.6 (e3). That the slow W_pg had been hiding this is argued from these two, not shown by itself.

**SP's queue (0): wrong, and part of the same.** The loads were to wait on SP only for a tile that PE frees; from 1290 to 1350 us SP waits mostly for landings instead. See the last section.

The sum: forecast -8, measured +11.5. Of the 19.5 between them the first phase makes 13.5, yA2 8.6 and the start-up 2.1; the gain, 1.6 larger than forecast, and the 3.3 us in yB and pp take 4.9 back.
